# A two-layer trunk on one core: where three pieces of side work are issued

## The chip, the cores and the metric

The kernel is one program on one core of a Trainium2 chip. Its engines are TensorE (PE, with the weight loads PEld beside it), VectorE (DVE), ScalarE (ACT), GpSimd (POOL) and SyncE (SP), which only issues DMAs and waits. The metric is the device time of the program in microseconds (us); three runs of the kernel before took 2968.97, 2973.52 and 2977.79 us, and their median, 2973.52 us, is the time before. About 0.3% of it, 8.9 us, is what a measurement of this kernel can tell from no change.

## What is computed

The input is 1024 rows of width 1024 in float32. There are two layers. Layer 0 mixes with a gated delta net, layer 1 with retention; after each mixer comes a gated feed-forward block of hidden width 2816 with a causal convolution of three taps. All of it is modulated by vectors made of a condition `c`:

```python
e = jax.nn.silu(c @ cond_w + cond_b)
for i in range(DEPTH):
    mod = (e @ ada_w[i] + ada_b[i])[:, None, :]
    sh1, sc1, g1, sh2, sc2, g2 = jnp.split(mod, 6, axis=-1)
    y = mixers[i % N_MIXERS](x * (1.0 + sc1) + sh1)
    x = layer_norm(DN_ALPHA * x + (1.0 + g1) * y, ln_g[i, 0], ln_b[i, 0])
    y = conv_ffn(x * (1.0 + sc2) + sh2, ffn_up[i], ffn_conv_w[i], ffn_conv_b[i], ffn_down[i])
    x = layer_norm(DN_ALPHA * x + (1.0 + g2) * y, ln_g[i, 1], ln_b[i, 1])
```

Retention has four heads. Its queries and keys are turned by a rotary embedding, the heads are processed in eight chunks of 128 rows with a running state, and each head's output is normalised and multiplied by `silu(gate)` before the output projection.

## The kernel before

**Products.** Every float32 operand of a product is split in two (`split`, lines 88 to 90): ACT copies it to a rounded high part (L89), DVE subtracts that from the operand to get the low part (L90), and PE makes three matmuls of 128x128 by 128x512 (high by low, low by high, high by high). So each block that PE is to multiply costs one ACT and one DVE instruction first, and a late L90 stops PE.

**Strassen-Winograd.** Large projections use seven block products instead of eight. For the projections into the feed-forward block and into retention's queries, keys and gates this is `strassen`: a list of items, each a pair of weight tiles, each finished by a `sink` that takes the four output quarters. `wino` computes an item: its sums of weight blocks are DVE instructions (L1213), the weights come by two SP DMAs (L1219, L1220) into the two buffers of the tag `wr`. For retention the first two items are gates and are computed directly; the other fourteen go through `wino`. A rotary item (`rope_item`) ends in twelve DVE instructions (L1651 to L1656) and stores to `qd`; a gate item (`gate_item`) ends in a SiLU on ACT and stores to `gd`. In the kernel before the list is two gates, eight rotary items, six gates.

**The down projections.** `proj_gen` (with `gate` None) computes the feed-forward block's output projection, once for each layer, as seven products, each of eleven steps j. The order is: 11 by 11, S1 by T1, S2 by T2, S4 by 22, 12 by 21, S3 by T3, 22 by T4, numbered p = 0 to 6. Each step loads an activation block (`ar`, SP, L1270) and a weight block (L1303), has both split (ACT L89, DVE L90), and PE makes twelve matmuls (L285 to L287, or L1437). The sums T1 to T4 are one more DVE instruction a step (L1311, L1314, L1317); products p = 0, 3 and 4 have none. The blocks S1 to S4 of the last pair of hidden features are made by POOL (L1585) at the end of the projection before.

**The residual rows.** The residual of a down projection is the stored, not yet scaled, normalised activation. `xload` loads four row tiles for the upper half of the rows during p = 2 and scales them on DVE (L1353). For the lower half `gain_half(n)`, n = 0 to 7, does one block of 128 rows by 512 columns: SP loads it (L1343), POOL multiplies by the layer-norm gain and adds the bias (L1345, two instructions), POOL issues the store to a buffer in memory (L1346) that `xload(1, t)` reads in p = 5 or later. `gain_half` takes its tile from the tag `lane` (four buffers) and is called in p = 0 and p = 1.

**Background blocks.** The modulation vectors are made in `bg_ada`: eight units, each a load of 512 KB of `ada_w` (`mvw`, SP, L214) and two DVE multiply-adds (L221, L223); every fourth unit ends in a matmul with ones (L245) and a DVE instruction (L246). Units wait in the list `bg`; each call of `bg_step` runs the work of the unit loaded at the last call, then starts the next unit's load. The tile comes from the tag named in `bg_tag`: `wr`, which the weights use too, or `lane` inside `strassen`. During the retention core, the eight units of `g1` of layer 1 are added when head 2 starts. `bg_gain` puts sixteen units ahead of them that scale the residual of the retention projection on POOL (L387 to L395).

**Order.** The program is scheduled when it is built: tiles from a tag are handed out in turn, and the scheduler orders each engine's instructions by a simulated timeline, so an instruction that is ready may be issued ahead of its place in the code. On the chip each engine's queue is then fixed, SP's DMAs included: an instruction that waits holds up all that stands behind it on its engine. In the retention core, `run` also fixes the order of PE's matmuls by a planner with its own latencies (`RL`).

Of the kernel before, what the change touches and what calls it, by code (L numbers as in the profile page):

```python
# [15 lines left out]
P = 128  # L16
D = 1024
S = 1024
# [15 lines left out]
def trunk_kernel(ctx: ExitStack, tc, A):  # L34
# [6 lines left out]
    dr = ctx.enter_context(tc.tile_pool(name="dr", bufs=1, space=bass.MemoryType.DRAM))  # L41

    BUFS = {"hTa": 8, "hTb": 8, "qkv": 20, "aux": 4, "auh": 8, "lane": 4, "cv": 4, "ada": 1,
            "wr": 2, "wh": 2, "wl": 2, "t2": 3, "sm": 14, "sm2": 6, "st": 8, "s8": 6, "S": 4, "qx": 3, "fs": 1, "xT": 4}
# [73 lines left out]

    def bg_step(tile=mm_tile):
        bg_ps[0] = tile  # L120
        if pend:
            pend.pop()()
        if bg:
            nxt = bg.pop(0)()
            if nxt:
                pend.append(nxt)

    def gemm_feat(src, hT_, step=True):
        w = load_w(src)
# [75 lines left out]
    def bg_ada(i, j, kind):  # L205
        box = {}

        def unit(nh, kp):
            if kp == 0:
                box["a"] = tl("ada", [P, HALF])  # L210
            a = box["a"]
            wr = tl(bg_tag[0], [P, 2, HALF], name="mvw")
            c0 = j * D + nh * HALF
            sp.dma_start(wr, A["ada_w"][i, kp * 256:(kp + 1) * 256, c0:c0 + HALF].rearrange("(a p) n -> p a n", p=P))  # L214
            return lambda: work(nh, kp, a, wr)

        def work(nh, kp, a, wr):
            for kk in range(2):
                k = kp * 2 + kk
                if k == 0:  # L220
# [156 lines left out]
    def bg_gain(n, src, dst):  # L377
        gb = []

        def unit(c, r):  # L380
            if r == 0:
                gb[:] = [tl("auh", [P, HALF], name="gb") for _ in range(2)]
                for t, nm in zip(gb, ("ln_g", "ln_b")):
                    sp.dma_start(t, A[nm][n:n + 1, hs(c)].to_broadcast([P, HALF]))
            x = tl("lane", [P, HALF], name="xg")
            rs = slice(r * P, r * P + P)
            sp.dma_start(x, src[rs, hs(c)])  # L387
            if r == 7:
                return gain(x, rs, c)
            return lambda: gain(x, rs, c)  # L390
# [883 lines left out]
    def proj_gen(nj, ablk, wsrc, slots, xsrc, G, final, ln_next, tag, ltags, dst, key, mm=pe.matmul, gate=None, gain=None):  # L1274
# [63 lines left out]

        def gain_half(n):
            hf, rs = n // 4, slice(HALF + n % 4 * P, HALF + (n % 4 + 1) * P)  # L1340
            x = tl("lane", [P, HALF], name="xg")
            with after("w"):
                sp.dma_start(x, gain[1][rs, hs(hf)])  # L1343
            for r, op in zip(grows, (ALU.mult, ALU.add)):
                pool.tensor_tensor(x, x, r[hf], op)  # L1345
            pool.dma_start(xsrc[rs, hs(hf)], x)  # L1346
# [100 lines left out]
        for p, (an, bn, fin, side, fresh) in enumerate(prods):  # L1447
# [8 lines left out]
            for j in range(nj):  # L1456
# [206 lines left out]
    def gate_item(u):  # L1663
        def start():
            def sink(q, a, b):
# [283 lines left out]
```

## Time and profile before

| | us |
|---|---|
| median of three runs (2968.97 to 2977.79) | 2973.52 |
| span of the profiled execution, first to last instruction | 2967.8 |
| PE busy | 2820.5 (95%) |
| DVE busy | 2242.4 (76%) |
| ACT busy | 1316.5 (44%) |
| POOL busy | 474.8 (16%) |
| down projection of layer 0, products 0 to 6 | about 1200 to 1412 |
| rotary items of the retention projection | about 1500 to 1655 |
| retention core | about 1785 to 2250 |
| down projection of layer 1, products 0 to 6 | about 2729 to 2949 |

The page gives the span and not a time of its own for the profiled execution; the span is 5.7 us below the median of the runs and 1.2 us below the fastest run. Places in the trace are given as us from the start of the span. A row of grouped instructions reads: line, engine, operation, tiles written and read, shapes, count, then busy time and mean duration in ns, then the idle time of the engine just before and what ended it. A row of waits reads: who waited, for whom, us in total, times, longest. A row of stages reads: the stretch, its length, then busy us of PE, PEld, DVE, ACT and POOL with counts, the granted clock of PE, the DMA engines' share, GB/s.

### The profile page before, as it was taken

Reading aid. Unit: us, or ns where it says so; the run is one execution under the profiler, and the core shown is the slowest. Engines: PE = TensorE matmul, PEld = TensorE weight load, DVE = VectorE, ACT = ScalarE, POOL = GpSimd, SP = SyncE. Lnnn points to the kernel's source line nnn. Section 1 sums busy time; section 2 is a strip of 40 time slices with the busy share of each in tenths; the row PEclk is TensorE's granted clock in tenths of the full one; section 3 lists DMA queues with packets and bytes.
Section 4 is the critical chain, followed back from the end, with each engine's and each line's share of the span. In section 5 each row is a group of like instructions: output and inputs, shape, how many; then the busy total and the mean of one; then the engine's idle time right before and its main releaser. Section 6 shows DMA issues by size and latency. Waiting matters only on the chain. (4 is left out here: it accounts for less than half of the span.)

```text
span 2967.8 us, 38939 instructions
## 1 busy us (share of the span) xinstructions
PE 2820.5 (95%) x13638; PEld 2304.5 (78%) x13638; DVE 2242.4 (76%) x4005; ACT 1316.5 (44%) x2413; POOL 474.8 (16%) x469
## 2 busy tenths in 40 slices
PE   8999898999999999999999999999999999999997
PEld 7887777887788888787877887777777788887786
DVE  5787787656688888879678645666689887777979
ACT  4744564444544444446433442222344544444443
POOL 0312221100001111610000202322202011112301
PEclk9999999999999999999999999999999999999998
DMA  7231222254245445865333544665664243335753
GB/s 275 79 113 65 86 79 79 83 167 160 91 158 163 158 151 174 305 198 179 120 128 117 181 160 152 203 189 175 205 212 157 91 135 107 107 107 176 274 183 137
DMA packets 244404, 451.01 MB, mean 152 GB/s; under 512 B 23088, under 2 KB 76592, under 8 KB 244208
## 3 DMA queue, kind: packets, MB, share of 16 engines
q1 hardware_dynamic: 213088, 401.07, 41.0%
q10 hardware_dynamic: 29760, 43.00, 4.0%
q0 software_dynamic: 1360, 4.46, 0.4%
q8 instruction: 107, 1.75, 0.3%
q14 instruction: 89, 0.73, 0.1%
HBM read 339.91 MB, written 108.53 MB: 151 GB/s over the span
## 5 line engine op out<-in xcount | busy, mean ns | idle before, releaser
L651 PE MATMUL acc<-hT,wh 128*128 128x512 f32 x960 | 299.3, 393 | 0.0
L1437 PE MATMUL acc<-bb,ab 128*128 128x512 f32 x984 | 231.4, 393 | 6.6 <-DVE bb L90 5.4
L1585 POOL TENSOR_TENSOR o<-o 128x512 f32<-128x512 f32 x80 | 110.7, 1394 | 716.4 <-DVE o L1578 490.8
L1437 PEld LDWEIGHTS acc<-bb,ab 128*128 128x128 f32 x984 | 182.6, 188 | 50.2 <-DVE bb L90 10.2
L1163 PE MATMUL acc<-T,wb 128*128 128x512 f32 x840 | 203.1, 391 | 6.7 <-DVE wb L90 6.7
L651 PEld LDWEIGHTS acc<-hT,wh 128*128 128x128 f32 x960 | 181.9, 190 | 34.1
L651 PE MATMUL acc<-hT,wl 128*128 128x512 f32 x480 | 201.1, 419 | 0.0
L89 ACT ACTIVATE ab<-ar 128x512 fp32r<-128x512 f32 x210 | 129.6, 625 | 152.7 <-PE mm L287 36.9
L90 DVE TENSOR_TENSOR ab<-ar,ab 128x512 fp32r<-128x512 f32 x210 | 161.9, 777 | 41.1 <-ACT ab L89 41.1
L1163 PEld LDWEIGHTS acc<-T,wb 128*128 128x128 f32 x840 | 157.0, 188 | 43.2 <-DVE wb L90 9.8
L90 DVE TENSOR_TENSOR wl<-wr,wh 128x1024 fp32r<-128x1024 f32 x95 | 119.7, 1260 | 69.6 <-ACT wh L89 68.6
L90 DVE TENSOR_TENSOR wb<-mm,wb 128x512 fp32r<-128x512 f32 x216 | 145.5, 682 | 31.2 <-ACT wb L89 30.6
L90 DVE TENSOR_TENSOR wb<-wr,wb 128x512 fp32r<-128x512 f32 x162 | 111.1, 691 | 69.8 <-ACT wb L89 69.1
L89 ACT ACTIVATE wh<-wr 128x1024 fp32r<-128x1024 f32 x95 | 100.7, 1061 | 132.3 <-PE acc L651 53.1
L1224 ACT ACTIVATE pc<-acc 128x512 f32<-128x512 f32 x143 | 84.9, 593 | 160.7 <-PE acc L1163 97.4
L1564 DVE SCALAR_TENSOR_TENSOR o<-g,vc,o 128x512 f32<-128x512 f32 (+2 forms) x176 | 145.4, 843 | 4.7 <-ACT o L1559 4.1
L89 ACT ACTIVATE wb<-mm 128x512 fp32r<-128x512 f32 x216 | 124.0, 595 | 51.9 <-DVE mm L1213 50.3
L89 ACT ACTIVATE wb<-wr 128x512 fp32r<-128x512 f32 x162 | 99.4, 628 | 104.0 <-DMA wr<-in_ffn_up 38.8
L651 PE MATMUL acc<-wh,hT 128*128 128x512 f32 x384 | 135.6, 415 | 1.6 <-DVE vv L90 1.6
L110 PE MATMUL acc<-T,wb 128*128 128x512 f32 x292 | 116.0, 397 | 9.4 <-DVE wb L90 9.4
L472 DVE SCALAR_TENSOR_TENSOR qkv<-raw,vc,qkv 128x512 f32<-128x512 f32 x144 | 111.6, 779 | 11.5 <-ACT qkv L470 10.7
L223 DVE SCALAR_TENSOR_TENSOR ada<-mvw,e,ada 128x512 f32<-128x512 f32 x140 | 106.9, 764 | 17.4 <-DMA mvw<-in_ada_w 17.1
(641 smaller groups left out, 7466.8 us busy)
## 6 DMA issues: line engine op xcount, KB each, us to landing
wr<-in_ffn_up SPq DMA_DIRECT2D x92, 512.0 KB, 4.4
mvw<-in_ada_w SPq DMA_DIRECT2D x80, 512.0 KB, 4.3
ad<-o SPq DMA_DIRECT2D x154, 256.0 KB, 3.1
ar<-ad SPq DMA_DIRECT2D x154, 256.0 KB, 3.9
Br<-in_ffn_down SPq DMA_DIRECT2D x88, 256.0 KB, 3.8
wr<-in_ret_wv SPq DMA_DIRECT2D x32, 512.0 KB, 3.9
ar<-od SPq DMA_DIRECT2D x56, 256.0 KB, 5.3
xs<-xt ACTq DMA_DIRECT2D x24, 512.0 KB, 3.7
```

Of the source, the lines that this page charges most:

```text
L89: act.activation(dst_h, src, AF.Copy)
L90: eng.tensor_tensor(dst_l, src, dst_h, ALU.subtract)
L110: mm(acc, wl[:, k], hl[0], start=first, stop=False)
L223: dve.scalar_tensor_tensor(a, wr[:, kk], e[:, k:k + 1], a, ALU.mult, ALU.add)
L472: dve.scalar_tensor_tensor(oh, raw[:, 3 - j:515 - j], w[:, 3 - j:4 - j], oh, ALU.mult, ALU.add)
L651: pq(pe.matmul(out, lhsT, rhs, start=start, stop=stop), cost)
L1163: return pe.matmul(*a, skip_group_check=True, **kw)
L1224: act.activation(t, X, AF.Copy)
L1437: return pe.matmul(*args, skip_group_check=True, **kw)
L1564: dve.scalar_tensor_tensor(tv, gv[:, c0 - j:c1 - j], w[:, 2 - j:3 - j], tv, ALU.mult, ALU.add)
L1585: (dve if fp == 0 else pool).tensor_tensor(o[d], o[x], o[y], op)
```

## The change

Three things change, and the buffer counts with them.

1. `gain_half` is called in p = 3 and p = 4 in place of p = 0 and p = 1, and takes its tile from the tag `xT`.
2. In the retention projection the twelve last items alternate: two direct gates, then rotary, rotary, gate, rotary, gate, rotary, gate, rotary, rotary, gate, rotary, gate, rotary, gate.
3. During the retention core `bg_tag` is `xT`. A unit started from there does its work two calls of `bg_step` after its load and not one; `pend` becomes a queue with a count for each entry. The accumulator tile `ada` is taken when the work starts and not when the load does.

The tag `xT` goes from four buffers of 512 columns (used at the start of the program for a few transposed tiles) to two of 2x512, the same memory.

```diff
-    ... "xT": 4}
+    ... "xT": 2}
...
     def bg_step(tile=mm_tile):
         bg_ps[0] = tile
-        if pend:
-            pend.pop()()
+        for p in pend:
+            p[0] -= 1
+        while pend and (pend[0][0] <= 0 or not bg):
+            pend.pop(0)[1]()
+            if not bg:
+                break
         if bg:
             nxt = bg.pop(0)()
             if nxt:
-                pend.append(nxt)
+                pend.append(list(nxt))
...
         def unit(nh, kp):
+            wr = tl(bg_tag[0], [P, 2, HALF], name="mvw")
+            c0 = j * D + nh * HALF
+            sp.dma_start(wr, A["ada_w"][i, kp * 256:(kp + 1) * 256, c0:c0 + HALF].rearrange("(a p) n -> p a n", p=P))
+            return 2 if bg_tag[0] == "xT" else 1, lambda: work(nh, kp, wr)
+
+        def work(nh, kp, wr):
             if kp == 0:
                 box["a"] = tl("ada", [P, HALF])
             a = box["a"]
-            wr = tl(bg_tag[0], [P, 2, HALF], name="mvw")
-            c0 = j * D + nh * HALF
-            sp.dma_start(wr, A["ada_w"][i, kp * 256:(kp + 1) * 256, c0:c0 + HALF].rearrange("(a p) n -> p a n", p=P))
-            return lambda: work(nh, kp, a, wr)
...
         def gain_half(n):
             hf, rs = n // 4, slice(HALF + n % 4 * P, HALF + (n % 4 + 1) * P)
-            x = tl("lane", [P, HALF], name="xg")
+            x = tl("xT", [P, HALF], name="xg")
...
-                if gain and p < 2 and j % 2 == 0 and p * 4 + j // 2 < 8 and j < 8:
-                    gain_half(p * 4 + j // 2)
+                if gain and p in (3, 4) and j % 2 == 0 and j < 8:
+                    gain_half((p - 3) * 4 + j // 2)
...
-    B = strassen(h0, xts, sc_r, sh_r, [gate_item(0), gate_item(2)]
-                 + [rope_item(h, j) for h in range(RH) for j in range(2)] + [gate_item(u) for u in range(4, 16, 2)], ("hTa", "aux", "qkv", "qkv", "hTa"), True)
+    ropes = [rope_item(h, j) for h in range(RH) for j in range(2)]
+    gates_ = [gate_item(u) for u in range(4, 16, 2)]
+    mixed = [ropes.pop(0)] + [r for k in range(3) for r in (ropes.pop(0), gates_.pop(0))] + [ropes.pop(0)]
+    mixed += [r for k in range(3) for r in (ropes.pop(0), gates_.pop(0))]
+    B = strassen(h0, xts, sc_r, sh_r, [gate_item(0), gate_item(2)] + mixed, ("hTa", "aux", "qkv", "qkv", "hTa"), True)
...
     free["qkv"] = 20
+    bg_tag[0] = "xT"
     run([(0.0, ret_fill())] + [(-1.0, core(h)) for h in range(RH)])
+    bg_tag[0] = "wr"
     layer_tail(1, mix, None, xs[1], xs[2], A["out"], None, True)
```

More of the change, by code (lines that the diff above doesn't have):

```diff
@@ L43, in trunk_kernel @@
     BUFS = {"hTa": 8, "hTb": 8, "qkv": 20, "aux": 4, "auh": 8, "lane": 4, "cv": 4, "ada": 1,
-            "wr": 2, "wh": 2, "wl": 2, "t2": 3, "sm": 14, "sm2": 6, "st": 8, "s8": 6, "S": 4, "qx": 3, "fs": 1, "xT": 4}
+            "wr": 2, "wh": 2, "wl": 2, "t2": 3, "sm": 14, "sm2": 6, "st": 8, "s8": 6, "S": 4, "qx": 3, "fs": 1, "xT": 2}
     def tl(tag, shape, dt=F32, name=None):
@@ L211, in unit @@
             a = box["a"]
-            wr = tl(bg_tag[0], [P, 2, HALF], name="mvw")
-            c0 = j * D + nh * HALF
-            sp.dma_start(wr, A["ada_w"][i, kp * 256:(kp + 1) * 256, c0:c0 + HALF].rearrange("(a p) n -> p a n", p=P))
-            return lambda: work(nh, kp, a, wr)
-        def work(nh, kp, a, wr):
             for kk in range(2):
@@ L389, in unit @@
                 return gain(x, rs, c)
-            return lambda: gain(x, rs, c)
+            return 1, lambda: gain(x, rs, c)
         def gain(x, rs, c):
```

## The prediction

> **What bounds the kernel now.** I read the page's first part, then the stages with PE's busy time, then who PE waited for in the stages that the diff touches.
>
> ```profile
> span 2967.8 us, 38939 instructions
> PE 2820.5 (95%) x13638; PEld 2304.5 (78%) x13638; DVE 2242.4 (76%) x4005; ACT 1316.5 (44%) x2413; POOL 474.8 (16%) x469
> ```
>
> PE is the bound: only 2967.8 - 2820.5 = 147 us of the span are without a matmul, so side work that moves can win or lose only by PE's gaps. The stages (products p of the first down projection in order, two stretches of the retention projection, a stretch of the retention core, the start of the second down projection):
>
> ```profile
> 1200.00:1231.00 31.00, 24.00 (x95) 18.45 (x94) 29.86 (x34) 16.12 (x36) 26.64 (x17) 0.94 1.04 391
> 1231.00:1261.00 30.00, 30.00 (x134) 24.82 (x134) 28.25 (x38) 14.94 (x27) 22.21 (x10) 1.00 0.84 293
> 1261.00:1291.00 30.00, 30.00 (x134) 24.86 (x133) 28.26 (x44) 14.99 (x28) 14.03 (x3) 1.00 0.62 206
> 1291.00:1321.00 30.00, 30.00 (x134) 24.85 (x133) 15.62 (x25) 14.94 (x28) 0.00 (x0) 1.00 0.68 211
> 1321.00:1350.00 29.00, 29.00 (x129) 24.01 (x128) 25.76 (x42) 8.97 (x16) 0.00 (x0) 1.00 0.50 159
> 1350.00:1380.00 30.00, 28.24 (x124) 22.32 (x124) 25.46 (x53) 14.05 (x23) 3.60 (x4) 1.00 0.54 168
> ...
> 1480.00:1500.00 20.00, 19.97 (x88) 16.09 (x87) 14.52 (x23) 8.41 (x16) 0.00 (x0) 1.00 0.19 66
> 1500.00:1655.00 155.00, 147.00 (x639) 119.09 (x638) 129.09 (x208) 47.41 (x85) 2.64 (x3) 1.00 0.41 137
> ...
> 1925.00:2035.00 110.00, 100.29 (x443) 75.92 (x442) 71.77 (x131) 21.94 (x36) 21.79 (x31) 0.98 0.59 177
> 2729.00:2753.00 24.00, 18.36 (x71) 13.49 (x70) 21.68 (x18) 10.71 (x19) 20.69 (x17) 0.94 1.04 387
> ```
>
> PE idles 7.0 us in the first product of layer 0 and 5.6 us in that of layer 1, both with DVE nearly full, POOL busy and the DMA engines full; in p = 3 (1291 to 1321) DVE has 14.4 us free and PE no gap. In the rotary items PE idles 8.0 us, in the stretch of the core 9.7.
>
> **Part 1, the residual rows leave p = 0 and 1.** Who PE waits for there, and what DVE and POOL do (1200 to 1220):
>
> ```profile
> PE acc L285 <- DVE ab L90: 7.0, 4, 2.8
> ```
>
> ```profile
> L90 DVE TENSOR_TENSOR ab<-ar,ab 128x512 fp32r<-128x512 f32 x4 | 9.1, 2296 | 3.4 <-ACT ab L89 3.4
> L90 DVE TENSOR_TENSOR bb<-Bw,bb 128x512 fp32r<-128x512 f32 x6 | 3.9, 679 | 0.0
> L260 DVE TENSOR_TENSOR fh<-fh,v 128x8 f32<-128x8 f32 x1 | 3.8, 3839 | 0.0
> ```
>
> ```profile
> L1345 POOL TENSOR_TENSOR xg<-xg,rowb 128x512 f32<-128x512 f32 x8 | 11.2, 1401 | 30.8 <-DMA Bw<-in_ffn_down 30.6
> L1585 POOL TENSOR_TENSOR o<-o 128x512 f32<-128x512 f32 x4 | 5.1, 1276 | 0.0
> ```
>
> The same split takes DVE 679 ns undisturbed and 2296 ns on average while POOL runs; a tiny L260 takes 3839. So DVE loses 4 x 1.6 + 3.8 = 10.3 us beside twelve POOL instructions, of which eight are residual rows and four the last blocks S (L1585), which stay. The port goes both ways; where DVE is dense, POOL starves:
>
> ```profile
> 1222.32 14.47 POOL L1345 TENSOR_TENSOR xg<-xg,rowb 128x512 f32<-128x512 f32 x2 [3.82 <-DMA xg<-xs]
> ...
> 1252.13 22.40 POOL L1345 TENSOR_TENSOR xg<-xg,rowb 128x512 f32<-128x512 f32 x2 [6.62 <-DMA xg<-xs]
> ```
>
> The Trainium skill, page "SBUF — State Buffer", section "Practical consequences", says the same: a DVE instruction with two SBUF inputs and a GpSimd instruction that reads SBUF exclude each other, and whichever starts first keeps the port for its whole instruction. By that rule the sixteen residual instructions block DVE as much in p = 3 and 4 as here, since the splits there have two SBUF inputs too; that is rival B, and the rows above agree with the rule.
>
> Layer 1, PE's waits (2725 to 2760), then DVE and POOL (2729 to 2753):
>
> ```profile
> PE acc L285 <- DVE ab L90: 4.9, 3, 2.6
> PE acc L286 <- DVE bb L90: 0.8, 2, 0.4
> ```
>
> ```profile
> L90 DVE TENSOR_TENSOR ab<-ar,ab 128x512 fp32r<-128x512 f32 x7 | 12.3, 1769 | 2.4 <-ACT ab L89 2.4
> L90 DVE TENSOR_TENSOR bb<-Bw,bb 128x512 fp32r<-128x512 f32 x7 | 9.0, 1307 | 0.0
> ```
>
> ```profile
> L1345 POOL TENSOR_TENSOR xg<-xg,rowb 128x512 f32<-128x512 f32 x9 | 13.8, 1535 | 31.1 <-DMA xg<-xs 30.9
> L1585 POOL TENSOR_TENSOR o<-o 128x512 f32<-128x512 f32 x4 | 5.6, 1394 | 0.4 <-DVE o L1578 0.4
> ```
>
> I leave PE the idle time in proportion to the POOL instructions that stay: 4 of 12 of 7.0 = 2.3, and 4 of 13 of 5.7 = 1.8. Gain 4.7 + 3.9 = 8.6 us. The granted clock is 0.94 in both stretches and 1.00 behind them; 6% of 24.0 and of 18.4 us are 1.4 and 1.1 us, and about two thirds of that goes with the gaps: 1.7 us. Together -10.3; bounds 0 (the S blocks alone hold DVE as long; they need the same data) and -15.2 (all of it). The eight loads and stores of 256 KB a projection also leave a stretch in which the DMA engines are full; I count nothing for that.
>
> What comes in p = 3 and 4: eight gains, sixteen POOL instructions of 1.3 us, at most 21 us of DVE's port a projection. In the built order of instructions SP issues the eight loads between the `ar` loads of p = 3 and 4, where it issued `xt` before, and SP runs a product ahead of PE, so POOL works from late p = 2 to p = 4. The cover is DVE's 14.4 us in p = 3, 3.2 in p = 4, and what DVE no longer loses in p = 0 and 1 (10 us), since it then is at the end of its three-deep buffers sooner; PE's three-deep splits cover single delays. 27 against 21: hidden, but not by much, and p = 5 has a gap of 1.7 us already. If the cover is gone, each POOL instruction costs about what it cost above, 7.0/12 = 0.6 us of PE: 16 x 0.6 = 9.3 a projection. I take +1 a projection, +2 (0 to 19).
>
> **Part 2, the mixed items.** PE's waits from 1480 to 1660, then PE at the change from rotary to gate:
>
> ```profile
> PE acc L1163 <- DVE wb L90: 5.3, 5, 1.1
> PE sc L1163 <- DVE wb L90: 2.7, 3, 1.1
> ```
>
> ```profile
> 1651.51 0.73 PE L1163 MATMUL acc<-T,wb 128*128 128x512 f32 x2 [1.06 <-DVE wb L90]
> ```
>
> Eight gaps, one behind each rotary item: its twelve DVE instructions stand in DVE's queue before the next item's split. The eighth, at 1651.51, falls into the gate item that follows the last rotary one, and is 1.06 us like those between two rotary items. In the built order the same DVE sequence stands behind each rotary item, whatever follows. So no backlog builds up that a gate could let DVE work off, and mixing removes nothing: 0. Bounds -8.0 (all eight gaps) and +2 (the end of the rotary items comes later, so POOL's `bg_gain` is moved from the gate items to the first values of the core, where PE has 128.9 of 130 us and DVE is half idle).
>
> **Part 3, the early blocks.** In the core before (1925 to 2035), PE's waits and what lies behind the longest:
>
> ```profile
> PE sc L651 <- DVE on L1780: 3.8, 3, 2.5
> PE sc L651 <- DVE Sr L1752: 3.5, 1, 3.5
> PE acc L651 <- DVE wl L90: 1.0, 2, 0.8
> ...
> DVE ada L223 <- DMA mvw<-in_ada_w: 12.0, 5, 4.9
> ```
>
> ```profile
> 1971.71 0.75 DVE L223 SCALAR_TENSOR_TENSOR ada<-mvw,e,ada 128x512 f32<-128x512 f32 x1 [4.42 <-DMA mvw<-in_ada_w]
> 1972.38 1.22 DVE L90 TENSOR_TENSOR wl<-wr,wh 128x1024 fp32r<-128x1024 f32 x1
> 1973.52 0.74 DVE L223 SCALAR_TENSOR_TENSOR ada<-mvw,e,ada 128x512 f32<-128x512 f32 x1
> 1974.18 1.28 DVE L1752 COPY Sr<-sc 128x512 f32<-128x512 f32 x2
> ```
>
> DVE stands 4.42 us before a block that has not landed; the weight split and the state copy behind it come late, and PE loses 3.5 us. In the built order six of the eight loads go far ahead: two into p = 4 and 5 of the layer-0 down projection, four among the weight loads at the start of the rotary items; four units' DVE work goes there too. The last two loads still follow the release of the two buffers inside the core. Removed for sure: 3.5 + 0.8. I take -5 with a part of the 3.8; bounds -9.7 (all gaps of the stretch) and +2 (the last two loads are waited for as now).
>
> What it costs where it goes: eight DVE instructions of 0.74 us (rows above), 5.9 us, in 1480 to 1500, where DVE has 20 - 14.5 = 5.5 us free. Two of the loads stand in SP's queue ahead of the weight loads of the second rotary item and wait for DVE's first units, so these weights come later. PE has no gap until the 0.6 us one in that item. Bounds 0 and +5.9; I take +2. L245 and L246 are only moved within the core, 0.
>
> **The sum.** -10.3 + 2 + 0 - 5 + 2 = -11.3 us: a span of 2956.5. The span of before is 5.7 us below the median of the runs; I keep that distance: 2973.5 - 11.3 = 2962.2 us, -0.38%. The bounds of the terms together, taken at half their width since they do not all come at once, make the forecast's own range 2954 to 2971.
>
> **The rivals.**
> - B, the contention follows: DVE loses in p = 3 to 5 what it gains in p = 0. Then part 1 is 0 and the rest is -3: 2970.5, no change. For it: the rule above, 25.8 of 29 us in p = 4. Against: PE had no gap in p = 1 and 2 although POOL worked there too (22.2 and 14.0 us).
> - C, slower: SP is blocked. `xT` has two buffers, so the third load waits until POOL has scaled and stored the first, and all `ar` and weight loads of p = 3 to 5 queue behind it. If DVE is dense then, POOL's pair takes 22.4 us as at 1252. It decides from the point where this wait exceeds SP's lead; if that is ten us a projection, 20 come on top and the gain is lost too: 2973.5 + 20 - 3 = 2990. For it: `xt` loads made SP wait 5.7 us there without harm, so there is a lead; it is the lead that is unknown. Against: DVE is not dense from 1291 on.
> - D, mixing works: a gate item gives DVE 5 us of slack, seven of the eight gaps go: 2962.2 - 7 = 2955. Against: the gap at 1651.51.
> - E, the early blocks only change their place: the delayed weights cost as much as the core wins: 2962.2 + 3 + 3 = 2968.
>
> ```profile
> SPq L280 <- DMA xg<-xg: 5.7, 1, 5.7
> ```
>
> **How the numbers follow.** Forecast 0.48, B 0.19, C 0.12, D 0.12, E 0.09. From the forecast down to D at 2953, up past B and E; C at 2990 is left out but for its mild cases: 2953 to 2977. Faster by over 0.3% (below 2964.6; 0.3% is about what a measurement of this kernel can tell from no change): 0.7 of the forecast and D, 0.46. Slower: C, 0.12. The rest, 0.42, within.
>
> **What would show it.** Part 1: in the first 31 us of each down projection PE idle about 2 us, POOL only four L1585, clock above 0.97; L1345 in p = 2 to 4, PE gaps there under 2 us. Wrong if PE waits for `bb` or `ab` there, or SP waits at L1343 for longer than PE's lead (C). Part 2: still eight gaps of about 1.06 us, each behind a rotary item. Part 3: L221 and L223 near 1480 to 1500, no wait of DVE for `mvw` over 2 us in the core, the gaps behind L1752 and `wl` gone, new gaps of some 2 us in the first two rotary items.

## The result and the profile after

The changed kernel took 2960.79 us, the median of five runs (2955.41 to 2968.07), and the kernel before 2973.8 us beside it: a ratio of 0.9958, with a 95% interval of 0.9943 to 0.9974. It is 0.4% faster. The forecast was 2962.2 us; the sum was right, but four of its terms were off by 3 to 11 us and cancelled. The two profiled executions, 2968.97 us before and 2955.50 after, are 14.1 us apart by their spans, the medians 13.0; the account below goes by the spans. The first lines of the page of the kernel after:

```profile
span 2953.7 us, 38896 instructions
PE 2816.4 (95%) x13638; PEld 2303.2 (78%) x13638; DVE 2243.3 (76%) x4005; ACT 1318.0 (45%) x2413; POOL 451.1 (15%) x469
```

Both programs have the same 13638 matmuls, so the time of the n-th one can be compared between the two traces. That gives the account by stretches (places in the trace of before, us; negative is time won):

| stretch | forecast | trace after |
|---|---|---|
| before the first down projection, 0 to 1200 (nothing changed there) | 0 | -3.4 |
| p = 0 of layer 0, then of layer 1 | -10.3 together | -9.8, -7.9 |
| p = 3 to 6 of layer 0, then of layer 1 | +2 together | +10.0, +2.9 |
| mixed items and start of the core, 1480 to 1830 | 0, and +2 for the blocks that come here | +5.0 |
| core, 1830 to 2035 | -5 | -14.5 |
| rest of the core, 2035 to 2320 | 0 | +3.9 |
| all else | 0 | -0.3 |
| sum | -11.3 | -14.1 |

Two rows need not be the change's. The first is a difference between two executions. The +3.9 stands as large in two kernels below that leave the core as it was (+4.1 in the mixing with gates left at the end, +4.2 without the multiplications). From 1830 to 2035 another such kernel (part 1 with four buffers) is 5.3 us longer than before, so differences of up to 5 us in the core are the noise of this account. The stretch 1925 to 2035 is steadier: -0.5 to +1.1 us in the six kernels below without part 3.

The stretches of the kernel after: length, then busy us of PE, PEld, DVE, ACT and POOL with counts, the granted clock of PE, the DMA engines' share, GB/s. They are p = 0, 3, 4 and 5 of layer 0, the stretch ahead of the rotary items, the first rotary items, the start of the core, its middle, and p = 0 of layer 1:

```profile
1196.00:1219.00 23.00, 23.00 (x104) 19.00 (x103) 22.95 (x34) 15.68 (x36) 6.33 (x4) 1.00 1.03 383
...
1279.00:1309.00 30.00, 30.00 (x134) 24.82 (x134) 16.50 (x19) 14.87 (x26) 14.96 (x14) 1.00 0.83 289
1309.00:1346.00 37.00, 30.02 (x127) 24.45 (x126) 28.15 (x46) 8.80 (x16) 0.00 (x0) 0.91 0.64 199
1346.00:1376.00 30.00, 27.13 (x121) 21.74 (x119) 25.00 (x53) 13.89 (x23) 4.82 (x4) 1.00 0.51 161
1477.00:1498.00 21.00, 20.91 (x91) 16.62 (x90) 19.64 (x33) 8.68 (x16) 0.00 (x0) 1.00 0.45 150
1498.00:1648.00 150.00, 146.28 (x641) 119.51 (x640) 107.52 (x173) 54.87 (x97) 0.00 (x0) 1.00 0.38 129
...
1730.00:1790.00 60.00, 54.94 (x230) 42.93 (x229) 31.12 (x39) 21.02 (x32) 15.68 (x11) 0.94 0.66 228
1917.00:2016.00 99.00, 98.84 (x450) 76.22 (x449) 64.26 (x119) 21.44 (x37) 20.10 (x28) 1.00 0.56 167
2713.00:2731.00 18.00, 17.76 (x79) 14.37 (x78) 11.20 (x16) 9.52 (x18) 3.25 (x2) 1.00 0.79 285
```

PE has no gap left in p = 0 of layer 0, 0.2 us in that of layer 1, and the clock is 1.00. In the core's middle it idles 0.2 us where it idled 9.7. But the stretch p = 4 now lasts 37 us with 30.02 of work, at a clock of 0.91, and PE idles 5 us at the start of the core.

What PE waits for in p = 4 of the kernel after, then the first instruction behind that wait, then DVE's instructions around it:

```profile
PE sc L289 <- DVE u L1414: 7.0, 1, 7.0
```

```profile
1322.24 0.77 PE L289 MATMUL sc<-bb,ab 128*128 128x512 f32 x1 [6.98 <-DVE u L1414]
```

```profile
1314.80 0.69 DVE L1321 TENSOR_TENSOR Br<-Bw,Br 128x512 f32<-128x512 f32 x1 [10.19 <-DMA Br<-in_ffn_down]
```

By the order of PE's matmuls, 132 a product, this one is the first of p = 4, and the gap stands between p = 3 and p = 4; the stretches that are named after products lie some 7 us early (in the kernel before p = 4 starts at 1328). DVE stands 10.19 us before a weight block that has not landed. It is the first block of p = 5, whose sum T3 (L1321) stands in DVE's built order ahead of the splits for p = 4. The instruction that would release PE's accumulator (L1414) stands behind it, at 1321.41. Who kept that load back shows on SP, its waits from 1240 to 1365 and then its last issues before the block:

```profile
SPq L1347 <- DMA xg<-xg: 19.8, 4, 7.4
SPq L1636 <- POOL xg L1349: 8.2, 3, 3.8
SPq L215 <- DMA xg<-xg: 2.2, 1, 2.2
```

```profile
1306.42 0.33 SPq L1636 DMA_DIRECT2D trig<-in_trig  x1
1309.06 0.38 SPq L215 DMA_DIRECT2D mvw<-in_ada_w  x1
1309.54 0.46 SPq L1307 DMA_DIRECT2D Br<-in_ffn_down  x1
```

Three kinds of load in SP's queue wait for the residual blocks: the next residual block, which needs one of the two buffers (L1347); the rotary tables (`trig`, L1636), which take the memory of POOL's gain and bias rows (`rowb`) when POOL is through with them; and the early background blocks (L215), which use the same `xT` buffers. The weight blocks of p = 4 and 5 queue behind them. The eleven of p = 4 were out by 1302.11; the first of p = 5 followed at 1309.54, after a table and a background block. (Lines of the kernel after are about four higher than those of before.)

### The profile page after: what moved, and what is told of

Same layout as the page of the kernel before. It is cut to its first block, busy times and chain, and to the rows that moved or that the text cites. A ratio compares the mean times of both kernels' runs of the same rounds, so it can differ in the third digit from the quotient of the medians.

```text
span 2953.7 us, 38896 instructions
## 1 busy us (share of the span) xinstructions
PE 2816.4 (95%) x13638; PEld 2303.2 (78%) x13638; DVE 2243.3 (76%) x4005; ACT 1318.0 (45%) x2413; POOL 451.1 (15%) x469
## 4 chain that ended last, share of the span: by engine, by line
PE 77%; DVE 9%; DMA 6%; ACT 4%; issue 2%; POOL 1%; SPq 0%; POOLq 0%; ACTq 0%; DVEq 0%
PE acc L655 15%; PE acc L1167 10%; PE acc L110 6%; PE acc L111 6%; PE acc L112 6%; PE sc L1167 5%; PE acc L1441 4%; PE sc L655 4%; PE mm L655 2%; PE sc L111 2%; PE sc L112 2%; PE sc L110 2%; PE mm L658 1%; DMA Br<-in_ffn_down 1%; PE acc L314 1%
## 5 line engine op out<-in xcount | busy, mean ns | idle before, releaser
L1441 PEld LDWEIGHTS acc<-bb,ab 128*128 128x128 f32 x984 | 183.7, 189 | 54.0 <-DVE bb L90 11.8
L1167 PE MATMUL acc<-T,wb 128*128 128x512 f32 x840 | 202.9, 390 | 6.5 <-DVE wb L90 6.5
L90 DVE TENSOR_TENSOR wl<-wr,wh 128x1024 fp32r<-128x1024 f32 x95 | 123.3, 1298 | 81.9 <-ACT wh L89 81.6
L90 DVE TENSOR_TENSOR ab<-ar,ab 128x512 fp32r<-128x512 f32 x210 | 159.7, 765 | 30.0 <-ACT ab L89 29.9
L90 DVE TENSOR_TENSOR wb<-mm,wb 128x512 fp32r<-128x512 f32 x216 | 146.0, 684 | 26.4 <-ACT wb L89 25.5
L90 DVE TENSOR_TENSOR wb<-wr,wb 128x512 fp32r<-128x512 f32 x162 | 110.5, 687 | 69.0 <-ACT wb L89 68.8
L110 PE MATMUL acc<-T,wb 128*128 128x512 f32 x292 | 115.6, 396 | 9.4 <-DVE wb L90 9.4
L476 DVE SCALAR_TENSOR_TENSOR qkv<-raw,vc,qkv 128x512 f32<-128x512 f32 x144 | 111.7, 780 | 11.4 <-ACT qkv L474 10.7
L111 PE MATMUL acc<-T,wb 128*128 128x512 f32 x292 | 115.1, 394 | 0.0
```

The source lines that it names most:

```text
L90: eng.tensor_tensor(dst_l, src, dst_h, ALU.subtract)
L110: mm(acc, wl[:, k], hl[0], start=first, stop=False)
L111: mm(acc, wh[:, k], hl[1], start=False, stop=False)
L476: dve.scalar_tensor_tensor(oh, raw[:, 3 - j:515 - j], w[:, 3 - j:4 - j], oh, ALU.mult, ALU.add)
L1167: return pe.matmul(*a, skip_group_check=True, **kw)
L1441: return pe.matmul(*args, skip_group_check=True, **kw)
```

## The experiments

Every ratio is against the kernel before, run beside on the same chip. Its medians were 2973.1 us (beside part 1 alone, the mixing alone, part 3 alone, and parts 1 and 3), 2971.24 (the mixing with gates at the end, the residual blocks without their arithmetic, and the two kernels with four buffers and the tables on SP), 2972.59 (part 1 with four buffers and the tables on POOL) and 2972.53 (the other three).

### Part 1 alone

```diff
-                if gain and p < 2 and j % 2 == 0 and p * 4 + j // 2 < 8 and j < 8:
-                    gain_half(p * 4 + j // 2)
+                if gain and p in (3, 4) and j % 2 == 0 and j < 8:
+                    gain_half((p - 3) * 4 + j // 2)
...
-            x = tl("lane", [P, HALF], name="xg")
+            x = tl("xT", [P, HALF], name="xg")
```

and `xT` with two buffers.

> The residual rows alone, in products p = 3 and 4 with two buffers. Theory: the gaps of p = 0 go (about -10 us in layer 0, -8 in layer 1, clock included), and in layer 0 the wait of SP for the two buffers comes back in p = 4 (+5 to +9 us); nothing changes in the core: 10 to 13 us faster. Rival: the +8.6 us of p = 4 comes from the two background loads that stand in SP's queue there in the changed kernel; without them the gap in p = 4 is under 2 us and the kernel is 16 us faster.

It took 2970.53 us (2958.55 to 2974.80, ten runs), a ratio of 0.9983 (0.9969 to 0.9996). By stretches p = 0 wins 9.7 and 7.9 us, and 1321 to 1350 loses 6.9. PE's wait in p = 4 and SP's:

```profile
PE sc L285 <- DVE u L1410: 5.0, 1, 5.0
```

```profile
SPq L1343 <- DMA xg<-xg: 19.6, 4, 7.1
...
SPq L1632 <- POOL xg L1345: 8.0, 4, 4.1
```

So the new wait comes with part 1, and needs no background block. The time is 2.6 us below the kernel before, where the theory said 10 to 13. The ten runs spread over 16 us, more than those of the kernel before; the profiled one took 2961.14 us, and where the others lose time no trace shows.

### The mixing alone

```diff
-    B = strassen(h0, xts, sc_r, sh_r, [gate_item(0), gate_item(2)]
...
+    mixed = [ropes.pop(0)] + [r for k in range(3) for r in (ropes.pop(0), gates_.pop(0))] + [ropes.pop(0)]
+    mixed += [r for k in range(3) for r in (ropes.pop(0), gates_.pop(0))]
```

> The mixed items alone. Theory: the gaps behind rotary items that follow a gate are 0.6 us in place of 1.06 (-2 us in all), and the start of the retention core pays for it with late loads and a lower clock (+5 to +7): 3 to 5 us slower. Rival, of the prediction: mixing changes nothing, and what was lost before the core has another cause: 0. Second rival: the core's gain (-14 us from 1830 to 2035) comes from POOL's residual work being moved by the mixing: then this kernel is 8 to 10 us faster.

It took 2977.52 us (2971.22 to 2981.22), a ratio of 1.0008 (0.9999 to 1.0018): no gain, by the medians 4.4 us more as the theory said, though the interval holds 1, and by its trace a loss of 6.5 us from 1480 to 1830. The gaps of the rotary items, each of which stands in the item behind, did shrink. Of the kernel before, the gap of the first rotary item (which follows a gate), then that of the second:

```profile
1508.67 0.50 PE L1163 MATMUL sc<-T,wb 128*128 128x512 f32 x1 [0.60 <-DVE wb L90]
...
1529.07 1.21 PE L1163 MATMUL acc<-T,wb 128*128 128x512 f32 x4 [1.06 <-DVE wb L90]
```

Of the kernel after, the gap of the second rotary item (which follows a rotary one), then that of the third (which follows a gate):

```profile
1526.33 0.97 PE L1167 MATMUL acc<-T,wb 128*128 128x512 f32 x3 [1.06 <-DVE wb L90]
...
1565.31 1.20 PE L1167 MATMUL sc<-T,wb 128*128 128x512 f32 x4 [0.61 <-DVE wb L90]
```

Each rotary item has its gap, of 0.6 us where a gate comes ahead of the item (0.83 the very first of the kernel after) and of 1.06 us where a rotary item does. PE's order tells how: at each gap of 0.6 us the rotary item ahead has its last product's twelve matmuls (L1163) issued two matmuls early, ahead of the end of the product before, and one early at the 0.83; none at the 1.06. Two matmuls are 0.45 us. In the kernel after the eight gaps sum to 6.0 us in place of 8.0. The loss is elsewhere: PE's waits of the mixing alone from 1740 to 1800,

```profile
PE mm L266 <- DMA xlo<-xs: 1.7, 1, 1.7
PE acc L651 <- DVE vv L90: 1.7, 2, 0.9
PE sc L1163 <- DVE wb L90: 1.6, 2, 1.0
PE acc L651 <- ACT wh L89: 1.1, 1, 1.1
PE acc L651 <- DVE wl L90: 0.5, 1, 0.5
```

around the start of the core, where before only one wait of 0.97 us stood, and a clock of 0.94 from 1730 to 1790 in place of 1.00. (0.6 us of these waits is the gap of the last rotary item, which the mixing brings here.)

### The mixing with three gates left at the end

```diff
-    B = strassen(h0, xts, sc_r, sh_r, [gate_item(0), gate_item(2)]
-                 + [rope_item(h, j) for h in range(RH) for j in range(2)] + [gate_item(u) for u in range(4, 16, 2)], ("hTa", "aux", "qkv", "qkv", "hTa"), True)
+    ropes = [rope_item(h, j) for h in range(RH) for j in range(2)]
+    gates_ = [gate_item(u) for u in range(4, 16, 2)]
+    mixed = [ropes.pop(0)] + [r for k in range(3) for r in (ropes.pop(0), gates_.pop(0))]
+    mixed += ropes + gates_
+    B = strassen(h0, xts, sc_r, sh_r, [gate_item(0), gate_item(2)] + mixed, ("hTa", "aux", "qkv", "qkv", "hTa"), True)
```

> The mixing alone, but with three gate items left at the end of the list (gates, rotary, rotary, gate, rotary, gate, rotary, gate, five... rotary in a row where they are left, then three gates). Mixing alone cost 6.5 us from 1480 to 1830 in its trace, although the gaps in the items shrank. Theory A (the loss is at the start of the core, where a rotary item now ends only one item ahead of it and DVE, ACT and the first loads of the core come late): with three gates behind the last rotary item the new gaps of 1750 to 1765 go, and the stretch 1480 to 1830 is 0 to 2 us shorter than in the kernel before; the gaps in the rotary items are 0.6 us behind a gate and 1.06 us behind another rotary item, 6.5 to 7.0 us together against 8.0. Theory B (the loss comes with mixing itself, by the order of loads that it gives): the stretch stays 4 us or more longer. In both the time lies within 0.3% of the kernel before, 2968 to 2978.

It took 2971.08 us (2968.63 to 2975.36), a ratio of 0.9999 (0.9989 to 1.0008), and from 1480 to 1830 it is 0.4 us shorter than before. The gaps of the eight rotary items sum to 6.6 us, as expected. The stretch 1730 to 1790 of the kernel before, of the mixing alone, and of this one:

```profile
1730.00:1790.00 60.00, 59.03 (x268) 48.42 (x268) 24.62 (x33) 25.34 (x40) 0.00 (x0) 1.00 0.50 168
```

```profile
1730.00:1790.00 60.00, 54.10 (x227) 42.23 (x225) 29.88 (x41) 20.32 (x32) 17.41 (x12) 0.94 0.66 220
```

```profile
1730.00:1790.00 60.00, 59.03 (x268) 48.47 (x267) 25.00 (x34) 25.93 (x41) 0.10 (x1) 1.00 0.56 184
```

With gates at the end the loss is gone, POOL's `bg_gain` is over before the core starts (0.10 us in place of 17.41), and theory A holds: the price of the mixing is a rotary item with only one gate between it and the core. Which of the things that come late there counts most (the loads, `bg_gain`, the first splits) was not told apart.

### Part 3 alone

```diff
+            return 2 if bg_tag[0] == "xT" else 1, lambda: work(nh, kp, wr)
...
+    bg_tag[0] = "xT"
     run([(0.0, ret_fill())] + [(-1.0, core(h)) for h in range(RH)])
+    bg_tag[0] = "wr"
```

and what belongs to it in `bg_step` and `bg_ada`, with `xT` of two buffers.

> The own early-loaded blocks alone. Theory: all the gain of the core is theirs, -10 to -14 us between 1830 and 2035, and about +1 where the early blocks go: 9 to 13 us faster. Rival: only the 4 to 5 us that stood behind waits for landed blocks: 3 to 5 us faster, the rest came from the mixing.

It took 2958.56 us (2955.0 to 2960.85), a ratio of 0.9944 (0.9930 to 0.9959), by itself as fast as the whole change, and 14.5 us below the kernel before. The stretch 1925 to 2035 is 10.7 us shorter; 1480 to 1655, where the moved work goes, costs 0.8. DVE's wait for a block in that stretch of the core, and the stretch 1479 to 1499:

```profile
DVE ada L227 <- DMA mvw<-in_ada_w: 1.2, 1, 1.2
```

```profile
1479.00:1499.00 20.00, 19.90 (x86) 15.78 (x86) 18.45 (x30) 7.92 (x14) 0.00 (x0) 1.00 0.45 147
```

DVE waited 12.0 us there before, in five waits. In all seven kernels with part 3 this stretch is 10.1 to 11.8 us shorter, which no kernel without it comes near. DVE's busy time ahead of the rotary items rises from 14.5 to 18.5 us of 20, and PE still idles only 0.1 us.

### Part 3 with the work one call behind its load

```diff
-            return 2 if bg_tag[0] == "xT" else 1, lambda: work(nh, kp, wr)
+            return 1, lambda: work(nh, kp, wr)
```

> Part 3 alone, with the work of a unit one call behind its load, as in the kernel before, and not two: only the own buffers are left of part 3. Theory (the loads waited for buffers that the weights hold; with own buffers six of the eight are made far ahead, whatever the delay): the stretch 1925 to 2035 stays 9 to 11 us shorter than before and the time is 2957 to 2961, as with the whole of part 3 (2958.56). Rival (it is the second call's delay that gives a load the time to land): DVE waits for mvw in the core again, 4 us or more at a time, half of the gain or more is lost, 2964 or more.

It took 2963.12 us (2960.01 to 2963.70), a ratio of 0.9961 (0.9946 to 0.9976). The stretch 1925 to 2035 is 10.1 us shorter than before, and DVE's wait:

```profile
DVE ada L227 <- DMA mvw<-in_ada_w: 2.0, 2, 1.5
```

So the own buffers make the gain in that stretch. The time lies between the two expectations, and the interval overlaps that of the whole part 3: whether the second call's delay is worth anything is left open.

### Parts 1 and 3, without the mixing

```diff
-    B = strassen(h0, xts, sc_r, sh_r, [gate_item(0), gate_item(2)] + mixed, ("hTa", "aux", "qkv", "qkv", "hTa"), True)
+    B = strassen(h0, xts, sc_r, sh_r, [gate_item(0), gate_item(2)]
+                 + [rope_item(h, j) for h in range(RH) for j in range(2)] + [gate_item(u) for u in range(4, 16, 2)], ("hTa", "aux", "qkv", "qkv", "hTa"), True)
```

> The change without the mixed items. Theory: 3 to 5 us faster than the whole change, -16 to -18 us against before, since the loss ahead of the core goes. Rival: the three parts do not add, and this is as fast as the whole change (-13) or slower.

It took 2957.92 us (2951.88 to 2966.74), a ratio of 0.9947 (0.9929 to 0.9965). That is 0.11% less than the whole change, on the side of the 5 us that the mixing costs by the trace, but the intervals overlap; against before it is 15.2 us, a little short of the theory's 16 to 18. The gap in p = 4 is 6.9 us.

### The residual blocks without their arithmetic

```diff
-            for r, op in zip(grows, (ALU.mult, ALU.add)):
-                pool.tensor_tensor(x, x, r[hf], op)
             pool.dma_start(xsrc[rs, hs(hf)], x)
```

in the kernel before.

> The kernel before without POOL's two multiplications and additions of each residual block (L1345): the blocks are loaded and stored in p = 0 and 1 as before, but left unscaled, so the lower half's residual lacks the layer-norm gain and bias. It asks what made PE wait in p = 0. Theory (POOL's instructions hold DVE's port): PE's gaps of 7.0 us in the first 31 us of the layer-0 projection and of 5.6 us in layer 1 fall under 1.5 us each, the means of L90 return to about 0.7 us, the stretches get about 9 and 8 us shorter, and the time falls by 13 to 18 us, to about 2957. Rival (the loads and stores, which fill the DMA engines, delay the activation and weight blocks): the gaps stay at 4 us or more each, L90 stays slow, and the time is 2970 to 2974.

It took 2955.28 us (2951.63 to 2955.47), a ratio of 0.9937 (0.9916 to 0.9958). PE's wait in p = 0 of layer 0, the stretch 1200 to 1231, and DVE's splits from 1195 to 1215:

```profile
PE acc L285 <- DVE ab L90: 1.9, 1, 1.9
```

```profile
1200.00:1231.00 31.00, 29.12 (x128) 23.77 (x128) 27.83 (x42) 18.35 (x40) 8.67 (x9) 1.00 1.04 393
```

```profile
L90 DVE TENSOR_TENSOR bb<-Bw,bb 128x512 fp32r<-128x512 f32 x9 | 8.1, 926 | 1.1 <-ACT bb L89 1.1
L90 DVE TENSOR_TENSOR ab<-ar,ab 128x512 fp32r<-128x512 f32 x8 | 7.1, 906 | 3.7 <-ACT ab L89 3.7
```

The DMA engines are as full as before (1.04, 393 GB/s), the loads and stores are all there, and the gap falls from 7.0 to 1.9 us, that of layer 1 from 5.6 to 1.2. The stretch is 7.6 us shorter (layer 1: 6.7). So it is POOL's arithmetic and not the transfers that made most of the wait in p = 0: 7.6 of the 9.8 us that the change wins there, 6.7 of 7.9 in layer 1. The gap that is left in layer 0 falls where two of the four L1585 that stay run, but in the kernel after the same four stay and PE has no gap; whether the rest, 2.2 and 1.2 us, belongs to them or to the transfers no run separates. The mean of L90 does not fall to 0.7 us but to 0.9.

### Part 1 with four buffers

`xT` keeps its four buffers of 512 columns in place of two of 2x512.

> Part 1 alone, as in the run of part 1 before it, but the residual blocks alternate over four tiles (the tag keeps its four buffers) and not two. It asks what made PE wait for 7 us in p = 4 of layer 0. Theory (a chain through two buffers: load, POOL, store, next load, with SP standing before the next load and the weight loads of p = 4 behind it): SP's 19.6 us of waiting for a store to land fall under 3 us, the gap in 1300 to 1350 falls under 2 us, that stretch loses 6 us or more against part 1 with two buffers, and the span falls from 2959.1 to about 2952. Rival (POOL and DVE fight for the port in p = 3 and 4): the gap stays at 5 us or more or moves into p = 3, and the span stays at 2957 to 2961.

It took 2960.87 us (2955.88 to 2965.04), a ratio of 0.9961 (0.9947 to 0.9975). The theory fell: the gap stays. PE's wait in p = 4, then SP's:

```profile
PE sc L285 <- DVE u L1410: 6.2, 1, 6.2
```

```profile
SPq L1632 <- POOL xg L1345: 18.7, 4, 12.3
```

SP no longer waits for a store of a residual block, but now stands 18.7 us before the rotary tables. The number was the rival's, but not its mechanism: SP is held just the same.

### Parts 1 and 3 with four buffers

```diff
-            x = tl("xT", [P, HALF], name="xg")
+            x = tl(("xT", "xG")[n % 2], [P, HALF], name="xg")
```

with `xG` of two buffers beside the `xT` of the change.

> Parts 1 and 3 without the mixing, and the residual blocks alternate over two pairs of buffers. Theory of the two-buffer chain: the 9.4 us that parts 1 and 3 with two buffers lose in 1321 to 1350 go, nothing else changes: 2957.9 - 8 = 2950. Rival of the port: 2956 to 2959. A third possibility: the four loads in flight and the early background loads meet in SP's queue, and the trigonometric rows, which wait for POOL's last use of the bias rows, hold SP all the same: a gap of 3 to 5 us stays, 2954.

It took 2954.62 us (2951.86 to 2960.51), a ratio of 0.9941 (0.9921 to 0.9962). The gap is 7.1 us, and SP stands 17.8 us before the tables and 5.9 before a background block: the third possibility, with the whole gap and not half of it.

### The rotary tables loaded by POOL

```diff
-                    sp.dma_start(t[hf], (A["trig"][i] if j else A["trigq"][h, i])[:, hs(hf)])
+                    pool.dma_start(t[hf], (A["trig"][i] if j else A["trigq"][h, i])[:, hs(hf)])
```

POOL reaches these loads after its own multiplications, so nobody stands before them. First in the kernel of parts 1 and 3 with four buffers:

> Parts 1 and 3 without the mixing, four buffers for the residual blocks, and the loads of the rotary tables (trig, L1636), which take the memory of POOL's gain and bias rows and so must wait for POOL's last multiplications, are issued by POOL and not by SP. With four buffers and these loads on SP the gap of 7 us in p = 4 stayed, with SP standing 17.8 us before them. Theory (SP, standing in order, keeps the weight loads of p = 4 back): SP no longer waits for POOL, DVE's 8 us wait for a weight block and PE's 7.1 us gap at 1322 fall under 2 us each, the stretch 1321 to 1350 costs at most 2 us against the kernel before in place of 9.9, and the time is 2945 to 2948. Rival (POOL holds the port in p = 3 and 4, SP only shows it): the gap stays at 5 us or more, 2953 to 2957.

It took 2954.36 us (2945.87 to 2955.72, five runs), a ratio of 0.9931 (0.9917 to 0.9945): the best of all kernels here, 0.27% below the whole change. Its trace is of an execution of 2945.87 us, 8 us below the median. The gap fell to 4.9 us, not under 2: by the gap almost, and by the time quite, this is what the rival of the port had said, so this kernel does not decide between them; part 1 with four buffers and the tables on POOL, below, does. SP's wait that is left:

```profile
SPq L215 <- DMA xg<-xg: 5.7, 2, 5.1
```

Then with two buffers:

> The same with two buffers for the residual blocks, as in the change: only the rotary tables leave SP. It tells the two holds on SP apart, the buffers (19.4 us of waiting in all, 7.3 the longest) and the tables (9.3 us, 4.5 the longest). If the tables are the hold that counts, the gap at 1322 falls under 2 us and the time is 2946 to 2949, as with four buffers; if the buffers are enough by themselves, 3 to 7 us of the gap stay and the time is 2951 to 2957.

It took 2959.17 us (2953.22 to 2966.18), a ratio of 0.9952 (0.9934 to 0.9970). The gap did not shrink, it doubled, which neither expectation allowed. PE's wait and SP's:

```profile
PE sc L289 <- DVE u L1414: 14.1, 1, 14.1
```

```profile
SPq L1347 <- DMA xg<-xg: 28.5, 5, 10.6
...
SPq L215 <- DMA xg<-xg: 8.7, 2, 6.8
```

With the tables out of the way SP comes to the next residual block sooner and stands there instead. Taking one hold away shifts SP's wait to the next. The trace of this kernel loses another 6.2 us from 1500 to 1655, most of it around one gap of 3.59 us behind the last rotary item; what made that is open.

### Part 1 with four buffers and the tables on POOL

> Part 1 alone with four buffers for the residual blocks and the rotary tables loaded by POOL: here no load in SP's queue between p = 2 and p = 5 waits for a residual block or its gain and bias rows, and no background block is loaded there. With parts 1 and 3 in this form SP still stood 5.1 us before a background block's load in p = 4, and PE's gap at 1322 was 4.9 us. Theory (what stands still in SP's queue makes the gap, whichever load it is): SP waits 0 us for xg, DVE waits under 2 us for a weight block in p = 4, the gap falls under 1.5 us, and 1321 to 1350 costs under 2 us against the kernel before, where part 1 with four buffers cost 7.9. Rival (the sixteen POOL instructions hold the port): the gap stays at 4 us or more although SP waits for nothing of POOL's. Time by the theory 2957 to 2962, by the rival 2960 to 2966.

It took 2956.42 us (2955.60 to 2959.84), a ratio of 0.9947 (0.9931 to 0.9964). No row of SP's waits from 1240 to 1365 names POOL or the store of a residual block any more. PE's wait in p = 4, DVE's, and the stretches p = 3 and 4:

```profile
PE sc L285 <- DVE u L1410: 1.0, 1, 1.0
```

```profile
DVE Br L1317 <- DMA Br<-in_ffn_down: 9.3, 7, 2.3
```

```profile
1280.00:1310.00 30.00, 30.00 (x134) 24.86 (x133) 25.10 (x23) 14.94 (x27) 20.76 (x21) 1.00 0.91 306
1310.00:1340.00 30.00, 28.99 (x128) 23.67 (x128) 26.37 (x44) 8.53 (x16) 0.00 (x0) 1.00 0.54 177
```

The gap is 1.0 us and 1321 to 1350 costs 1.3 us. DVE still waits 9.3 us for weight blocks, where the theory said under 2, but in seven waits of 2.3 us at most. POOL does the same sixteen instructions, and DVE's splits do pay for it (from 1281 to 1340):

```profile
L90 DVE TENSOR_TENSOR ab<-ar,ab 128x512 fp32r<-128x512 f32 x21 | 22.0, 1061 | 2.2 <-ACT ab L89 2.2
```

but PE has no gap in the stretch where POOL does them. The port is fought for, and covered. The eight kernels with part 1, by what SP waited in 1240 to 1365 for POOL or a store of a residual block, and by PE's gap in p = 4:

| kernel | SP's waits, us | gap, us |
|---|---|---|
| part 1, four buffers, tables on POOL | none | 1.0 |
| parts 1 and 3, four buffers, tables on POOL | 5.7 + 0.2 | 4.9 |
| part 1, four buffers | 18.7 | 6.2 |
| parts 1 and 3, four buffers | 17.8 + 5.9 | 7.1 |
| part 1, two buffers | 19.6 + 8.0 | 5.0 |
| the whole change | 19.8 + 8.2 + 2.2 | 7.0 |
| parts 1 and 3, two buffers | 19.4 + 9.3 + 3.5 | 6.9 |
| parts 1 and 3, two buffers, tables on POOL | 28.5 + 8.7 + 0.7 | 14.1 |

The gap goes with SP's holds at the two ends. In between it does not follow their sum (5.9 us of waits with a gap of 4.9, 27.6 with 5.0); that their place in the queue counts there is likely and not shown. The clean case is part 1 with four buffers: the tables' issuer alone takes the gap from 6.2 to 1.0 us. Parts 1 and 3 with all three holds gone was not tried, so for the whole change the cause is carried over from that case.

## Why the prediction was right, and where it was wrong

**What bounds the kernel, and part 1 in p = 0.** The mechanism was right: POOL's two-input arithmetic and DVE's splits hold each other up, and the transfers matter little (the run without the arithmetic; at most the 2.2 and 1.2 us that it leaves). The size was low. The step "I leave PE the idle time in proportion to the POOL instructions that stay" kept 2.3 and 1.8 us of gaps; the kernel without the arithmetic kept 1.9 and 1.2, the changed kernel 0 and 0.2. The sum of both p = 0 was -17.7 us and not -10.3, past the bound of -15.2. The term that was too small is the one for the clock. It took 6% of PE's busy time, 2.5 us, and two thirds of that. But the matmuls of the two stretches kept PE busy for 24.0 and 18.4 us before, and the same matmuls take 21.2 and 15.9 us after: 5.3 us, which with the gaps, 12.6 less 0.2 us, make up the 17.7. The 0.94 was the mean over the whole stretch; from 1215 to 1220 the clock was 0.72. How much of the 5.3 us is the clock, and how much is matmuls that start up anew behind a gap, was not separated.

**Part 1 in p = 3 to 6.** This step failed: +2 was +12.9, 10.0 of it in layer 0. "The cover is DVE's 14.4 us in p = 3" was right as far as the port goes. What came was rival C, SP blocked: in layer 0 at its price of "ten us a projection" (10.0), in layer 1 hardly (2.9). C erred only in that the gain of p = 0 would be lost too. The argument against it, "DVE is not dense from 1291 on", looked at how long POOL's pair takes. POOL's first pair and its fifth in the kernel after:

```profile
1253.14 10.30 POOL L1349 TENSOR_TENSOR xg<-xg,rowb 128x512 f32<-128x512 f32 x2 [42.48 <-DMA xg<-xs]
...
1289.55 3.04 POOL L1349 TENSOR_TENSOR xg<-xg,rowb 128x512 f32<-128x512 f32 x2 [8.94 <-DMA xg<-xs]
```

From the second pair on POOL is quick (3.01 us), and SP is held all the same: by the first pair and by the whole way of a block through its buffer, load and store included. And the wait that counted most with four buffers was one that the prediction did not see: the rotary tables wait for POOL's last multiplication with the rows whose memory they take. In layer 1, where no tables and no background blocks follow, p = 3 to 6 cost 2.9.

**Rival B** (the contention follows) is refuted: part 1 with SP freed keeps both gains of p = 0 (9.8 and 8.3 us) and pays 3.3 us in p = 3 to 6 of layer 0, 1.3 of them in 1321 to 1350, and 1.7 in layer 1. The Trainium skill, page "SBUF — State Buffer", section "Who interferes with whom", under its practical consequences, says that a DVE instruction with two SBUF inputs contends with a GpSimd instruction that reads SBUF. The trace agrees in p = 3 as in p = 0 (L90 takes 1061 ns on average there, 679 undisturbed), and the rule says nothing on whether PE feels it.

**Part 2.** Zero was wrong in both directions at once. "mixing removes nothing" (and with it the zero) failed: the gap is 1.06 us for a rotary item that follows another and 0.6 for one that follows a gate, so mixing wins 2.0 us, and the row that shows it, the first of the eight gaps at 1508.67, stood in the trace of before. What was read was the last of them, and what follows a rotary item indeed changes nothing. That no backlog builds up may still be right: the two sizes differ by two matmuls in PE's order, and not by what DVE has left to do. But the end of the list costs more than the bound of +2: with a rotary item one gate ahead of the core PE waits five times around its start and the clock falls. Net +5.0. Rival D (2955) is refuted.

**Part 3.** The mechanism was right, the size half: the stretch 1925 to 2035 won 10.4 us where the prediction took 5 and bounded it by 9.7, all of its gaps. The step that was mis-sized left the three waits for `on` (L1780), 3.8 us, in part to stay, and the other small gaps whole; in the kernel after PE idles 0.2 us there. The cost where the work goes, taken as +2, was 0.3 us in the whole change from 1480 to 1500 and 0.8 us up to 1655 in part 3 alone: DVE had the room, and in place of new gaps of some 2 us in the first two rotary items the one there was grew, from 0.60 to 0.83 us in the whole change and to 1.02 in part 3 alone. Rival E is refuted.

**The sum.** Part 1 gave 4.8 us in place of 8.3, part 2 took 5.0 in place of 0, part 3 gave 10.4 to 14.5 in place of 3. Errors of +3.5 and +5.0 us meet one of -7 to -11, and the time came out within 1.4 us of the forecast because they cancel: that is luck. By the medians even the 4.8 us of part 1 are not to be seen: part 3 alone stands at 0.9944, parts 1 and 3 at 0.9947, the whole change at 0.9958, with intervals that overlap. The range of 2954 to 2971 does not come out of its own working either: half the distance to the bounds of all terms gives 2951 to 2982.

## What to carry to other kernels

When a step is moved, list every instruction that uses memory that the step holds, also what comes after it in the same memory (here the tables behind the gain rows and the background blocks), and look where those stand in a queue that works in order; the move is free only if none of them stands ahead of what the bounding engine needs. A load that must wait for an engine can be issued by that engine's own queue, behind the work it waits for; this took the gap from 6.2 to 1.0 us where nothing else held SP, and from 6.9 to 14.1 where the next hold came up sooner. Of a repeated gap, read the odd one out first: here the first of eight, not much over half as long as the others, told that what comes ahead of a rotary item counts.

## What was not expected of the hardware

Gaps of about 1 us bring the clock down too. The start of the core in the kernel after, in 5 us steps around three gaps of 1.13, 1.08 and 0.47 us between 1753 and 1757:

```profile
1749.00:1754.00 5.00, 3.87 (x18) 2.76 (x16) 1.29 (x2) 0.71 (x2) 1.81 (x2) 1.00 0.96 315
1754.00:1759.00 5.00, 3.45 (x8) 2.29 (x9) 3.52 (x4) 3.72 (x5) 1.29 (x2) 0.62 1.01 366
1759.00:1764.00 5.00, 5.00 (x17) 3.90 (x16) 0.99 (x1) 0.00 (x0) 2.12 (x1) 0.69 1.05 406
```

By the granted clock, 0.62 over 3.45 and 0.69 over 5.00 busy us, 1.3 + 1.6 = 2.9 us were lost, about as much as the 2.7 us of the gaps themselves. The stretch behind the single gap of 7 us in p = 4:

```profile
1320.00:1325.00 5.00, 2.76 (x7) 2.22 (x8) 4.81 (x9) 0.00 (x0) 0.00 (x0) 0.50 0.59 189
```

That gap cost no more: 0.50 for 2.76 busy us, 1.4 us, and 0.98 to 1.00 from there on. So in these traces short gaps close together cost double, and a long one did not. Eight gaps of 0.6 to 1.06 us that stand some 20 us apart left the clock of the rotary items of before at 1.00.
